# Top-10 indices of 8192 rows: smaller chunks, keys in planes, merged gathers and an order by hand

## The chip, the cores and the metric

One core of a Trainium2 chip. The metric is the device time of one execution in microseconds (us), the median of the runs that a comparison made; the granted clock was 1.00. "Before" and "after" are the two kernels of the change. In the profile, SPq is the queue of SyncE, which issues the DMAs; DVE is VectorE, ACT is ScalarE, POOL is GpSimd.

## The reference

```python
x = np.random.randn(8192, 8192).astype(np.float32)      # k = 10
indices = np.argpartition(x, -k, axis=1)[:, -k:]
values = np.take_along_axis(x, indices, axis=1)
sorted_idx = np.argsort(-values, axis=1)
return np.take_along_axis(indices, sorted_idx, axis=1)  # 8192 x 10 indices, largest first
```

The input is 268 MB, read once; 64 tiles of 128 rows.

## The kernel before

Per tile: load 4 MB (two halves), convert to fp16 keys on ScalarE, fold each chunk of 16 keys to its maximum on VectorE, choose the 12 best chunks of 512, gather those chunks in fp32 on GpSimd, separate them, rank the 192 candidates. Each of the four gathers writes 768 values a row (the page's line L134): 16 sets of 3 chunks of 16, one set for each row of its group of 16, so each row needs only its own; sixteen small DMAs per tile pick it out.

```python
C = 16; G = 12; LAG = 2                                 # NCHUNK = 8192 // C
def load(t):                                            # cut: tile 0 in eight parts
    for h in range(2):
        nc.sync.dma_start(out=xt[:, h*w:(h+1)*w], in_=x[r0:r0+P, h*w:(h+1)*w])

def front(t):
    for h in range(2):
        kh = kpool.tile([P, H], fp16, tag="kh")
        nc.scalar.activation(out=kh, in_=xt[:, h*H:(h+1)*H], func=ACTF.Copy, bias=-CENTER)   # dense
        v = kh.rearrange("p (c w) -> p c w", w=C)
        n = C // 2
        while n > 1:                                    # folds in place, short runs
            nc.vector.tensor_tensor(out=v[:, :, 0:n], in0=v[:, :, 0:n], in1=v[:, :, n:2*n], op=ALU.max)
            n //= 2
        nc.vector.tensor_tensor(out=m[:, h*HC:(h+1)*HC], in0=v[:, :, 0], in1=v[:, :, 1], op=ALU.max)
    # choice: max, max_index, match_replace, max, max_index on m [128, 512]
    nc.scalar.activation(out=idx[:, :, 0:3], in_=cid[:, 0:G]..., func=ACTF.Copy, scale=float(C))
    gw = gwpool.tile([P, G, 16, C], fp32, tag="gw")
    for s in range(0, G, 3):                            # four gathers of 48 indices
        nc.gpsimd.indirect_copy(out=gw[:, s:s+3]..., data=xt..., idxs=idx[:, s//3, 0:3])
    for r in range(16):                                 # each row's own set, 8 partitions a copy
        nc.sync.dma_start(out=g[r::16, :, :], in_=gw[r::16, :, r, :])
# back(t): five VectorE instructions on g; every 8th tile decode() and one output DMA, on SyncE
for t in range(ntiles):                                 # the scheduler orders the rest
    load(t); front(t)
    if t >= LAG: back(t - LAG)
```

## Time and profile before

| | before |
|---|---|
| median (lowest to highest) | 1241.06 us (1240.95 to 1242.26, 3 runs) |
| busy share VectorE / ScalarE / GpSimd | 65% / 39% / 27% |
| mean load rate | 217 GB/s; 359 GB/s while a load runs |
| mean time from load to load, SyncE's timeline, 54.27 to 1169.18 us | 18.9 us |

The busy shares alone say nothing here: no engine is full. In a wait line the three numbers are the total us, the number of times and the longest.

### The profile page before, as it was taken

How to read it: one execution, taken by the hardware profiler on the slowest of the kernel's cores; microseconds unless marked ns; L12 is line 12 of the kernel's file. 1: busy time of each engine (PE TensorE's matmuls, PEld its weight loads, DVE VectorE, ACT ScalarE, POOL GpSimd, SP SyncE). 2: the span in 40 equal slices, each digit the busy share in tenths (PEclk: the TensorE clock that was granted, in tenths of full speed). 3: DMA queues.
4: the chain of work that ended last, by engine and by line, in shares of the span. 5: the costliest groups of instructions: out<-in, count | busy, mean ns of one | idle time of the engine just before them, and what ended most of it. 6: DMA issues, size and time to landing. Idle time of an engine off the chain costs nothing.

```text
span 1241.8 us, 4178 instructions
## 1 busy us (share of the span) xinstructions
PE 0.2 (0%) x2; PEld 0.1 (0%) x2; DVE 804.0 (65%) x1589; ACT 478.9 (39%) x199; POOL 339.0 (27%) x263
## 2 busy tenths in 40 slices
PE   0000000000000000000000000000000000000000
PEld 0000000000000000000000000000000000000000
DVE  5866666766766657666676567756667576685642
ACT  6344343343343443333443433424433334334310
POOL 0222223222222222222232222222222223223221
DMA  9656656557556566465575575565664765656610
GB/s 393 236 204 263 235 199 259 201 217 275 215 203 258 192 242 257 167 270 217 208 269 200 218 274 207 212 234 201 258 255 164 276 222 202 267 180 239 265 17 8
DMA packets 134146, 275.70 MB, mean 222 GB/s; under 512 B 116960, under 2 KB 116960, under 8 KB 117984
## 3 DMA queue, kind: packets, MB, share of 16 engines
q1 hardware_dynamic: 134112, 275.42, 59.8%
q14 instruction: 34, 0.28, 0.1%
HBM read 268.44 MB, written 0.66 MB: 217 GB/s over the span
## 4 chain that ended last, share of the span: by engine, by line
DMA 54%; SPq 29%; DVE 8%; issue 5%; ACT 2%; POOL 1%; POOLq 0%; DVEq 0%; PE 0%; ACTq 0%
DMA xt<-in_x_dram 54%; SPq L142 27%; ACT kh L95 2%; SPq L80 2%; DVE kh L103 2%; DVE pick L178 1%; DVE hot L170 1%; POOL gw L134 1%; DVE cidb L119 0%; DVE hot L174 0%; DVE wall L122 0%; DVE wall L118 0%; DVE m L120 0%; DVE m L107 0%; DVE posb L155 0%
## 5 line engine op out<-in xcount | busy, mean ns | idle before, releaser
L103 DVE TENSOR_TENSOR kh<-kh 128x2048 f16<-128x2048 f16 (+2 forms) x384 | 342.2, 891 | 377.4 <-ACT kh L95 368.7
L134 POOL INDIRECT_COPY gw<-xt,idx 128x768 f32 x256 | 338.3, 1322 | 880.5 <-issue 630.0
L95 ACT ACTIVATE kh<-xt 128x4096 f16<-128x4096 f32 (+1 forms) x134 | 464.2, 3464 | 267.8 <-DMA xt<-in_x_dram 267.7
L127 ACT ACTIVATE idx<-cidb 128x12 uint16<-128x12 uint16 x64 | 13.7, 214 | 445.2 <-DVE cidb L123 445.2
L107 DVE TENSOR_TENSOR m<-kh 128x256 f16<-128x256 f16 x128 | 85.8, 671 | 4.4
L122 DVE MAX8 wall<-m 128x8 f16<-128x512 f16 x64 | 44.5, 695 | 2.2
L118 DVE MAX8 wall<-m 128x8 f16<-128x512 f16 x64 | 44.5, 695 | 2.2
L151 DVE MAX8 t8a<-g 128x8 f32<-128x192 f32 x64 | 22.0, 344 | 33.8 <-DMA g<-gw 33.5
L119 DVE FIND_INDEX8 cidb<-wall,m 128x8 uint16<-128x512 f16 x64 | 43.8, 685 | 0.0
L123 DVE FIND_INDEX8 cidb<-wall,m 128x8 uint16<-128x512 f16 x64 | 43.8, 685 | 0.0
L120 DVE MATCH_REPLACE8 m<-wall,m 128x512 f16<-128x512 f16 x64 | 43.2, 676 | 0.0
L154 DVE MAX8 t8b<-g 128x8 f32<-128x192 f32 x64 | 23.1, 361 | 2.2
L155 DVE FIND_INDEX8 posb<-t8b,g 128x8 uint16<-128x192 f32 x64 | 22.5, 352 | 0.0
L152 DVE FIND_INDEX8 posb<-t8a,g 128x8 uint16<-128x192 f32 x64 | 22.5, 352 | 0.0
L153 DVE MATCH_REPLACE8 g<-t8a,g 128x192 f32<-128x192 f32 x64 | 21.9, 343 | 0.0
L170 DVE TENSOR_TENSOR hot<-slot,slots 128x960 f16<-128x960 uint16 x8 | 9.5, 1190 | 0.0
L178 DVE TENSOR_REDUCE pick<-hot 128x80 f32<-128x960 f16 x8 | 9.2, 1153 | 0.3
L155 DVE MATCH_VALUE_LOAD posb<-t8b,g 128x8 f32 x64 | 5.9, 92 | 2.2
L123 DVE MATCH_VALUE_LOAD cidb<-wall,m 128x8 f16 x64 | 5.9, 92 | 2.2
L152 DVE MATCH_VALUE_LOAD posb<-t8a,g 128x8 f32 x64 | 5.9, 92 | 2.2
L119 DVE MATCH_VALUE_LOAD cidb<-wall,m 128x8 f16 x64 | 5.9, 92 | 2.2
L174 DVE TENSOR_TENSOR hot<-hot,cidb 128x960 f16<-128x960 f16 x8 | 5.8, 722 | 0.3
(19 smaller groups left out, 21.7 us busy)
## 6 DMA issues: line engine op xcount, KB each, us to landing
xt<-in_x_dram SPq DMA_DIRECT2D x126, 2048.0 KB
g<-gw SPq DMA_DIRECT2D x1024, 6.0 KB
xt<-in_x_dram SPq DMA_DIRECT2D x8, 512.0 KB
out_dram<-opack SPq DMA_DIRECT2D x8, 80.0 KB
```

What stands on the lines that cost most here:

```text
L95: nc.scalar.activation(out=kh[:, q * w:(q + 1) * w], in_=xt[:, h * H + q * w:h * H + (q + 1) * w], func=ACTF.Copy, bias=-CENTER, scale=1.0,)
L103: nc.vector.tensor_tensor(out=v[:, :, 0:n], in0=v[:, :, 0:n], in1=v[:, :, n:2 * n], op=ALU.max)
L107: nc.vector.tensor_tensor(out=m[:, h * HC:(h + 1) * HC], in0=v[:, :, 0], in1=v[:, :, 1], op=ALU.max)
L118: nc.vector.max(out=w16[:, 0:8], in_=m)
L119: nc.vector.max_index(out=cid[:, 0:8], in_max=w16[:, 0:8], in_values=m)
L120: nc.vector.match_replace(out=m2, in_to_replace=w16[:, 0:8], in_values=m, imm_value=KEY_MIN)
L122: nc.vector.max(out=w16[:, 8:16], in_=m2)
L123: nc.vector.max_index(out=cid[:, 8:16], in_max=w16[:, 8:16], in_values=m2)
L134: nc.gpsimd.indirect_copy(out=gw[:, s:s + per, :, :].rearrange("p s r w -> p (s r) w"), data=xt.rearrange("p (c w) -> p c w", w=C), idxs=i ...
L142: nc.sync.dma_start(out=g[r::16, :, :], in_=gw[r::16, :, r, :])
L152: nc.vector.max_index(out=pos[:, 0:8], in_max=t8a, in_values=g)
L155: nc.vector.max_index(out=pos[:, 8:16], in_max=t8b, in_values=g2)
```

## The change

Its intent: chunks of 8 halve the candidates to rank and the words that a gather reads; keys stored plane by plane (all first elements, then all second ones) make every fold one contiguous run; two gathers replace four; the gather buffer is laid out so that each row's set is one run; the output DMA leaves SyncE's queue; and the order is set by hand, with the next tile's conversion ahead of this tile's index. The cut leaves out the numbers of buffers: the key buffers go from three half tiles to two whole ones, and the small tiles from three buffers to two.

```diff
-C = 16
+C = 8
+PER = 6
-            ... kh = kpool.tile([P, H], fp16), converted dense, in two halves, folded in place
+        khs[t] = kpool.tile([P, C, NCHUNK], fp16, tag="kh", name="kh")
+            nc.scalar.activation(
+                out=khs[t][:, :, h * w // C:(h + 1) * w // C],
+                in_=xt[:, h * w:(h + 1) * w].rearrange("p (c w) -> p w c", w=C),
+                func=ACTF.Copy, bias=-CENTER, scale=1.0)
+        n = N // 2                                     # fold(t)
+        while n >= NCHUNK:
+            nc.vector.tensor_tensor(out=kh[:, 0:n], in0=kh[:, 0:n], in1=kh[:, n:2 * n], op=ALU.max)
+            n //= 2
-        gw = gwpool.tile([P, G, 16, C], fp32, tag="gw")           # four gathers
+        gw = gwpool.tile([P, 16, G, C], fp32, tag="gw")
+        for a in range(G // PER):                                 # two gathers of 96 indices
+            ... mybir.InstIndirectCopy(..., num_valid_indices=16 * PER)
-            nc.sync.dma_start(out=g[r::16, :, :], in_=gw[r::16, :, r, :])
+            nc.sync.dma_start(out=gs[t][r::16, :], in_=gw[r::16, r, :, :]...)
-        nc.sync.dma_start(out=out_tpn...)
+        nc.scalar.dma_start(out=out_tpn...)
+    with tc.manual_schedule():
+        for t in range(3): load(t)
+        convert(0)
+        for t in range(ntiles + LAG):
+            if t < ntiles:
+                fold(t); choose(t)
+                if t + 1 < ntiles: convert(t + 1)
+                index(t)                               # ScalarE, behind convert(t + 1)
+                gather(t)                              # two gathers, then 16 copies on SyncE
+                if t + 3 < ntiles: load(t + 3)         # SyncE, behind the copies of t
+            if t >= LAG: rank(t - LAG)
```

More of the change, by code (lines that the diff above doesn't have):

```diff
@@ L50 @@
     consts = ctx.enter_context(tc.tile_pool(name="consts", bufs=1))
-    kpool = ctx.enter_context(tc.tile_pool(name="keys", bufs=3))
+    kpool = ctx.enter_context(tc.tile_pool(name="keys", bufs=2))
     gwpool = ctx.enter_context(tc.tile_pool(name="gw", bufs=2))
-    small = ctx.enter_context(tc.tile_pool(name="small", bufs=3))
+    small = ctx.enter_context(tc.tile_pool(name="small", bufs=2))
     bpool = ctx.enter_context(tc.tile_pool(name="batch", bufs=2))
@@ L69 @@
         nc.gpsimd.memset(o, 0)
-    st = {}
-    batch = {}
+    xts, khs, gs, idxs, batch = {}, {}, {}, {}, {}
+    H = N // 2
     def load(t):
-        xt = xpool.tile([P, N], fp32, tag="xt")
+        xts[t] = xpool.tile([P, N], fp32, tag="xt", name="xt")
         r0 = t * P
@@ L80, in load, with convert, fold, choose @@
             nc.sync.dma_start(
-                out=xt[:, h * w:(h + 1) * w], in_=x[r0:r0 + P, h * w:(h + 1) * w]
+                out=xts[t][:, h * w:(h + 1) * w], in_=x[r0:r0 + P, h * w:(h + 1) * w]
             )
-        st[t] = {"xt": xt}
-    def front(t):
-        xt = st[t]["xt"]
-        m = small.tile([P, NCHUNK], fp16, tag="m")
-        H = N // 2
-        HC = NCHUNK // 2
-        for h in range(2):
-            kh = kpool.tile([P, H], fp16, tag="kh")
-            nparts = 4 if t == 0 else 1
-            w = H // nparts
-            for q in range(nparts):
-                nc.scalar.activation(
-                    out=kh[:, q * w:(q + 1) * w],
-                    in_=xt[:, h * H + q * w:h * H + (q + 1) * w],
-                    func=ACTF.Copy, bias=-CENTER, scale=1.0,
-                )
-            v = kh.rearrange("p (c w) -> p c w", w=C)
-            n = C // 2
-            while n > 1:
-                nc.vector.tensor_tensor(
-                    out=v[:, :, 0:n], in0=v[:, :, 0:n], in1=v[:, :, n:2 * n], op=ALU.max
-                )
-                n //= 2
+    def convert(t):
+        xt = xts[t]
+        khs[t] = kpool.tile([P, C, NCHUNK], fp16, tag="kh", name="kh")
+        nparts = 8 if t == 0 else 2
+        w = N // nparts
+        for h in range(nparts):
+            nc.scalar.activation(
+                out=khs[t][:, :, h * w // C:(h + 1) * w // C],
+                in_=xt[:, h * w:(h + 1) * w].rearrange("p (c w) -> p w c", w=C),
+                func=ACTF.Copy, bias=-CENTER, scale=1.0,
+            )
+    def fold(t):
+        kh = khs[t].rearrange("p w c -> p (w c)")
+        n = N // 2
+        while n >= NCHUNK:
             nc.vector.tensor_tensor(
-                out=m[:, h * HC:(h + 1) * HC], in0=v[:, :, 0], in1=v[:, :, 1], op=ALU.max
+                out=kh[:, 0:n], in0=kh[:, 0:n], in1=kh[:, n:2 * n], op=ALU.max
             )
+            n //= 2
+    def choose(t):
+        m = khs.pop(t)[:, 0, :]
         if t % TB == 0:
@@ L116, in front @@
         w16 = wall[:, t, :]
-        m2 = small.tile([P, NCHUNK], fp16, tag="m2")
         nc.vector.max(out=w16[:, 0:8], in_=m)
         nc.vector.max_index(out=cid[:, 0:8], in_max=w16[:, 0:8], in_values=m)
+        m2 = small.tile([P, NCHUNK], fp16, tag="m2")
         nc.vector.match_replace(out=m2, in_to_replace=w16[:, 0:8], in_values=m,
@@ L123, in front, with index, gather, rank @@
         nc.vector.max_index(out=cid[:, 8:16], in_max=w16[:, 8:16], in_values=m2)
-        per = 3
-        idx = small.tile([P, G // per, 4], u16, tag="idx")
+    def index(t):
+        cid = batch[t // TB][0][:, t % TB, :]
+        idxs[t] = small.tile([P, G // PER, 8], u16, tag="idx", name="idx")
         nc.scalar.activation(
-            out=idx[:, :, 0:per],
-            in_=cid[:, 0:G].rearrange("p (a b) -> p a b", b=per),
+            out=idxs[t][:, :, 0:PER],
+            in_=cid[:, 0:G].rearrange("p (a b) -> p a b", b=PER),
             func=ACTF.Copy, scale=float(C),
         )
-        gw = gwpool.tile([P, G, 16, C], fp32, tag="gw")
-        for s in range(0, G, per):
-            nc.gpsimd.indirect_copy(
-                out=gw[:, s:s + per, :, :].rearrange("p s r w -> p (s r) w"),
-                data=xt.rearrange("p (c w) -> p c w", w=C),
-                idxs=idx[:, s // per, 0:per],
-                i_know_this_is_slow=True,
+    def gather(t):
+        gw = gwpool.tile([P, 16, G, C], fp32, tag="gw")
+        for a in range(G // PER):
+            runs = gw[:, :, a * PER:(a + 1) * PER, :].rearrange("p r s w -> p s r w")
+            nc.gpsimd.add_instruction(
+                mybir.InstIndirectCopy(
+                    name=nc.get_next_instruction_name(),
+                    ins=[nc.gpsimd.lower_ap(xts[t]), nc.gpsimd.lower_ap(idxs[t][:, a, 0:PER])],
+                    outs=[nc.gpsimd.lower_ap(runs)],
+                    num_valid_indices=16 * PER,
+                )
             )
-        g = small.tile([P, G, C], fp32, tag="g")
+        gs[t] = small.tile([P, G * C], fp32, tag="g", name="g")
         for r in range(16):
-            nc.sync.dma_start(out=g[r::16, :, :], in_=gw[r::16, :, r, :])
-        st[t]["g"] = g
-    def back(t):
-        g = st.pop(t)["g"].rearrange("p s w -> p (s w)")
+            nc.sync.dma_start(
+                out=gs[t][r::16, :], in_=gw[r::16, r, :, :].rearrange("p s w -> p (s w)")
+            )
+        del xts[t], idxs[t]
+    def rank(t):
+        g = gs.pop(t)
         pos = batch[t // TB][1][:, t % TB, :]
@@ L182, in decode @@
         )
-        nc.sync.dma_start(
+        nc.scalar.dma_start(
             out=out_tpn[:, b * TB:(b + 1) * TB, :],
@@ L186, in decode @@
         )
-    for t in range(ntiles):
-        load(t)
-        front(t)
-        if t >= LAG:
-            back(t - LAG)
-    for t in range(ntiles - LAG, ntiles):
-        back(t)
+    with tc.manual_schedule():
+        for t in range(3):
+            load(t)
+        convert(0)
+        for t in range(ntiles + LAG):
+            if t < ntiles:
+                fold(t)
+                choose(t)
+                if t + 1 < ntiles:
+                    convert(t + 1)
+                index(t)
+                gather(t)
+                if t + 3 < ntiles:
+                    load(t + 3)
+            if t >= LAG:
+                rank(t - LAG)
     tie = small.tile([P, ntiles], fp32, tag="tie")
```

## The prediction

> **What bounds the kernel now.** I read the page first: the busy shares, then the chain that ended last, because no engine is near full.
>
> ```profile
> PE 0.2 (0%) x2; PEld 0.1 (0%) x2; DVE 804.0 (65%) x1589; ACT 478.9 (39%) x199; POOL 339.0 (27%) x263
> ...
> DMA 54%; SPq 29%; DVE 8%; issue 5%; ACT 2%; POOL 1%; POOLq 0%; DVEq 0%; PE 0%; ACTq 0%
> ```
>
> VectorE is idle a third of the time and the chain is made of input loads (54%) and of SyncE's own queue (29%), so this is a loop between the loads and the queue that issues them. Next, the timeline of SyncE over one of the 64 tiles:
>
> ```profile
> 601.03 0.86 SPq L80 DMA_DIRECT2D xt<-in_x_dram  x2
> 602.00 17.05 SPq L142 DMA_DIRECT2D g<-gw  x16
> 619.16 0.86 SPq L80 DMA_DIRECT2D xt<-in_x_dram  x2
> ```
>
> From one pair of loads to the next is 18.1 us. The chain of waits over the same stretch says why 16 small copies take 17 us:
>
> ```profile
> 601.46 11.83 DMA xt<-in_x_dram
> 613.29 0.02 issue
> 613.30 0.60 SPq L142
> 613.90 0.04 issue
> ...
> 618.45 0.60 SPq L142
> 619.05 0.06 issue
> ```
>
> [...]copies 7 and 8 after a load pair wait for the two halves of that load. SyncE issues seven copies in the load's shadow, waits until it lands (613.29), then issues nine more at 0.643 us, and only then the next load. The period is 12.3 (load issue to landing) + 9 x 0.643 + about 0.1 = 18.2. The same two stretches, by windows (us, then busy time of each engine, clock, DMA share, GB/s):
>
> ```profile
> 601.50:613.30 11.80, 0.00 (x0) 0.00 (x0) 7.35 (x19) 3.83 (x2) 3.80 (x3) 1.00 0.93 359
> 613.30:619.60 6.30, 0.00 (x0) 0.00 (x0) 4.69 (x6) 3.62 (x1) 1.25 (x1) 1.00 0.09 8
> ```
>
> Full rate while the load runs, 8 GB/s while nine copies are issued: bandwidth is not the limit. Finally the instructions that the change touches, from the groups with shapes kept apart:
>
> ```profile
> L95 ACT ACTIVATE kh<-xt 128x4096 f16<-128x4096 f32 x126 | 455.7, 3617 | 263.8 <-DMA xt<-in_x_dram 263.7
> L134 POOL INDIRECT_COPY gw<-xt,idx 128x768 f32 x256 | 338.3, 1322 | 880.5 <-issue 630.0 <-DMA g<-gw 248.3 <-ACT idx L127 2.2
> L103 DVE TENSOR_TENSOR kh<-kh 128x2048 f16<-128x2048 f16 x128 | 161.3, 1260 | 368.7 <-ACT kh L95 368.7
> ...
> L107 DVE TENSOR_TENSOR m<-kh 128x256 f16<-128x256 f16 x128 | 85.8, 671 | 4.4
> L122 DVE MAX8 wall<-m 128x8 f16<-128x512 f16 x64 | 44.5, 695 | 2.2
> ...
> L154 DVE MAX8 t8b<-g 128x8 f32<-128x192 f32 x64 | 23.1, 361 | 2.2
> ```
>
> An indirect_copy shows 1.3 us busy but 2.2 us of "issue" before it. In the timeline of the tail, where nothing else runs, four of them start at 1208.43, 1211.89, 1215.35 and 1218.81: one costs 3.46 us, so a tile's four 13.8 us.
>
> [...] The trace agrees that 8-partition copies are the dear ones:
>
> ```profile
> L142 SPq DMA_DIRECT2D g<-gw x1024: 589/599/5939, 43.9 to 1229.8; - x171
> L183 SPq DMA_DIRECT2D out_dram<-opack x8: 394/394/411, 194.7 to 1237.5; - x8
> ```
>
> The output copy has 1,024 runs of 80 bytes and costs 0.394 us of issue; the separating copy has 96 runs and costs 0.599. Runs do not set the issue cost. [...]L107 reads one fp16 per 32 bytes and takes 671 ns for 256 elements, where the dense rate seen in MAX8 ((695-361)/(512-192), about 1.04 ns an element) would add only 267 ns to an overhead of some 150 ns[...]. [...]the gap before an indirect_copy grows from 2.2 to 3.8 us where folds run. [...]
>
> **The change part by part.**
> (1) Folds. [...]2048 outputs take 1.26 us now, so 4096 take 1.26+1.07 = 2.33, 1024 take 0.73; sum 4.3 us a tile, against 2 x (1.260+0.742+0.671+0.671) = 6.7. Saves 2.4.
> (2) Chunk choice. 1024 maxima instead of 512: five instructions, each 512 x 1.04 = 0.53 us longer: +2.7. Ranking has 96 elements instead of 192: 5 x -0.1 = -0.5. VectorE's work a tile stays near 12.6 us (804/64) and it is not the bound.
> (3) Conversion. ScalarE now reads fp32 with a step of 32 bytes[...]. Dense: 3.617 = 0.20 + 4096 x 0.833 ns. [...]0.20 + 4096 x 1.667 = 7.0 us a half. I give this three chances in four.
> (4) Gathers. Two instructions with 96 indices of 8 elements: the written 768 elements stay, 1.26 us each. The 2.2 us gap stays if it is a cost per instruction and becomes 4.4 if per index; I choose the middle, 3.3. Two cost 2 x (3.3+1.26) = 9.1 us instead of 13.8.
> (5) Separation. Still 16 copies over 8 partitions: I keep 0.643 us each. 96 runs become 8, which only lightens DMA work that the 359 GB/s shows to be harmless.
> (6) Output copy on ScalarE's queue. SyncE's waits list 76.9 us for VectorE's decode. Counting load pairs, 54.3 to 1169.2 us holds 59 periods, mean 18.9; the plain ones are 18.1 to 18.8, so some 4 us for each of seven batches, about 30 us, is really saved.
> (7) Order. This is the part I fear. The manual order puts the index instruction of tile t behind the conversion of t+1 on ScalarE, and the load of t+3 behind the copies of t on SyncE. So load(t+1), conversion(t+1), index(t), gathers(t), copies(t), load(t+3) is one chain over two periods. Before, the index came straight after the choice, the gathers ran beside a whole load, and four tiles were prefetched, not three. Moreover fold(t+1) starts at the same moment as gathers(t) and holds them off: 4.3 us, less about 1.1 us which the gather seems to get done first (at 22.02 the index is there, the folds end at 25.45, writing starts at 26.58, only 1.1 later), so about 3.0.
>
> Two periods are: the first half's conversion starts 7.4 us after the load's issue (608.39-601.03), two conversions 14.1, index 0.3, gathers 3.0+9.1, 16 copies 10.3, waits 0.2: 44.4 us, so 22.2 us a tile. Head: conversion of tile 0 in eight pieces of 1.9 ends at 20, of tile 1 at 34, gathers 46, copies and load(3) at 56.5. Then 60 periods, 1332. Tail from the last load: conversion 21.5, index 21.8, gathers of the last two tiles 33.9 and 43.0, copies to 54.5, landing 1.8, ranking to end 10.1 as now: 66. Sum 56.5+1332+66 = 1455.
>
> **Rivals.** (a) ScalarE reads at full rate. Then conversion ends 12.3+3.7 after the load's issue, and two periods are 16.0+0.4+12.1+10.5 = 39.0, 19.5 a tile; head 49, tail 61: 1280. For it: the conversion writes densely and reads one stream. Against: L107.
> (b) The gather gap is a cost per instruction (2.2). That takes 2 x 1.1 us off two periods: 21.1 a tile and about 1385; with (a) 18.4, close to the queue bound, about 1210.
> (c) The queue bound of 12.3 + 9 copies stays the only limit and the batches' stalls go: 18.2 x 60 + head 49 + tail 61 = 1202. It needs both (a) and (b).
> (d) Longer runs cut the issue of a copy to 0.39 us. Sixteen save 3.3 us in two periods: 1455 becomes 1355, and (c) would fall to some 16.3 a tile, near 1090. Against: the output copy above.
> (e) The gap is fully per index (4.4): 23.3 a tile, about 1525.
>
> **Range and chances.** Strided ScalarE at 3 in 4 spans 1385 to 1525; dense ScalarE mostly 1210 to 1310. I put the time a little under the main sum, 1430, because several small rivals pull down and one up; 1250 to 1510 should hold it 8 times in 10. Faster needs two or three rivals at once: 0.10. Within 2%: 0.13. Slower: 0.77.
>
> **What would show it.** The conversion's mean for 4096 elements (7.0 or 3.6 us); the start-to-start time of the two indirect_copies without folds (4.6, or 3.5, or 5.7); the issue of a separating copy (0.60 or 0.39); SyncE waiting mainly for GpSimd and no longer for loads; load pairs alternating short and long with a mean near 22 us; the index waiting on ScalarE's own order. A dense conversion makes the number wrong; SyncE still waiting for the loads makes the mechanism wrong.

The marked cuts here and in the expectations are what no trace or run of this case shows. No term of the sum goes with them: two periods still come to 44.4 us and the whole to 1455. What is left rests on the traces as follows.

- That copies 7 and 8 wait for the two halves of a load is in SyncE's timeline: after the load pair of 601.03, copy 6 starts at 605.24, copy 7 at 608.33 and copy 8 at 613.30, with two waits for the load in between, 4.0 us in all. What in the queue makes them wait is not shown.
- The folds' 1.07 us for 2048 more outputs is an estimate: about twice the step from 1024 to 2048 outputs, 742 to 1260 ns.
- The 7.0 us is an estimate too, under an "if": that ScalarE pays twice its dense 0.833 ns for each element, as L107 on VectorE takes (671 - 150)/256 = 2.03 ns an element against MAX8's 1.04. The 150 ns are rounded from 695 - 512 x 1.04 = 162.

## The result, and the profile after

| | before | after |
|---|---|---|
| median | 1241.66 us (4 runs) | 1491.24 us (4 runs, 1490.61 to 1491.63) |
| ratio, 95% interval | | 1.2003 (1.1978 to 1.2027) |
| VectorE / ScalarE / GpSimd busy | 65% / 39% / 27% | 53% / 65% / 10% |
| mean time from load to load | 18.9 us | 22.8 us |

A ratio here is the mean time of one kernel's runs over that of the other's of the same rounds, so not quite the ratio of the medians. The mean time from load to load is the last issue of a load pair less an early one in SyncE's timeline, over the pairs between (after: 1423.37 - 75.97 us over 59).

From the page of the changed kernel, the busy line and the chain that ended last:

```profile
PE 0.2 (0%) x2; PEld 0.1 (0%) x2; DVE 787.5 (53%) x1269; ACT 968.3 (65%) x199; POOL 147.0 (10%) x135
...
SPq 37%; issue 31%; DMA 20%; POOL 9%; DVE 1%; ACT 1%; POOLq 0%; DVEq 0%; PE 0%; ACTq 0%
```

The loads' own share of the chain fell from 54% to 17% (the page's line list; the other 3% of DMA are copies landing): what now fills it is the copies' issue (SPq) and the gathers with the unshown part in front of them (issue and POOL). ScalarE has 1% of this chain, so the profile does not put the conversion on it; that the conversion is on the path is read from the times below and shown by experiment 1. What SyncE waits for says the same, from its queue's waits:

```profile
SPq L146 <- POOL gw L136: 766.7, 63, 38.6
...
SPq L146 <- DMA xt<-in_x_dram: 3.7, 2, 2.8
```

Before, it waited 181 us for loads and 101 us for GpSimd; now 4 and 767. The queue's old bound, copies 7 and 8 waiting for a load to land, hardly binds any more. Two periods of the timeline of the changed kernel, from one load pair to the second one after it (start, duration, engine, line, operation):

```profile
603.92 0.85 SPq L81 DMA_DIRECT2D xt<-in_x_dram  x2
...
611.34 14.96 ACT L91 ACTIVATE kh<-xt 128x4096 f16<-128x4096 f32 x2 [10.56 <-DMA xt<-in_x_dram]
...
626.21 0.20 ACT L126 ACTIVATE idx<-cidb 128x12 uint16<-128x12 uint16 x1
626.34 4.28 DVE L101 TENSOR_TENSOR kh<-kh 128x4096 f16<-128x4096 f16 x3 [13.57 <-ACT kh L91]
...
633.71 1.14 POOL L136 INDIRECT_COPY gw<-xt,idx 128x768 f32 x1 [19.70 <-issue]
...
638.49 1.15 POOL L136 INDIRECT_COPY gw<-xt,idx 128x768 f32 x1 [3.64 <-issue]
639.66 9.63 SPq L146 DMA_DIRECT2D g<-gw  x16
...
649.40 0.85 SPq L81 DMA_DIRECT2D xt<-in_x_dram  x2
```

Read it downwards: each step begins where the one above ends (the L101 line is no step of the chain: it is the fold that starts with the index). The load leads to the conversion of tile t+1, that to the index of tile t (whose choice had been ready since 611), that to the gathers, those to the copies, those to the next load but one: 649.40 - 603.92 = 45.5 us for two tiles. The shown part of the first gather, which I take to be its writing, starts 7.3 us after the index ends (626.41), that of the second only 3.64 after the first: the fold that starts with the index held the first back. Experiment 2 has the control: no fold runs there between the index and the next gather, and the wait is 3.8 us. Note that the profile calls the 19.70 us "issue": it shows no wait, though the index had come only 7.3 us before. As the prediction said they would, the load pairs alternate short and long: 18 to 21 us and 25 to 28.

The groups with shapes kept apart, after:

```profile
L91 ACT ACTIVATE kh<-xt 128x4096 f16<-128x4096 f32 x126 | 945.2, 7552 | 475.2 <-DMA xt<-in_x_dram 475.2
L101 DVE TENSOR_TENSOR kh<-kh 128x4096 f16<-128x4096 f16 x64 | 146.7, 2293 | 655.7 <-ACT kh L91 655.7
L136 POOL INDIRECT_COPY gw<-xt,idx 128x768 f32 x128 | 146.3, 1143 | 1321.8 <-issue 1293.5 <-DMA xt<-in_x_dram 24.5 <-DVE posb L161 3.8
```

The strided conversion takes 7.55 us a half against 3.62; the largest fold and the gather's shown part are as cheap as hoped.

### The profile page after: what moved, and what is told of

The parts are those of the page before. It is cut to its first block, busy times and chain, and to the rows that moved or that the text cites. A ratio compares the mean times of both kernels' runs of the same rounds, so it can differ in the third digit from the quotient of the medians.

```text
span 1489.7 us, 3606 instructions
## 1 busy us (share of the span) xinstructions
PE 0.2 (0%) x2; PEld 0.1 (0%) x2; DVE 787.5 (53%) x1269; ACT 968.3 (65%) x199; POOL 147.0 (10%) x135
## 4 chain that ended last, share of the span: by engine, by line
SPq 37%; issue 31%; DMA 20%; POOL 9%; DVE 1%; ACT 1%; POOLq 0%; DVEq 0%; PE 0%; ACTq 0%
SPq L146 37%; DMA xt<-in_x_dram 17%; POOL gw L136 9%; DMA g<-gw 3%; ACT kh L91 1%; SPq L81 0%; DVE kh L101 0%; POOLq L136 0%; DVE cidb L116 0%; DVE wall L120 0%; DVE wall L115 0%; DVE m L118 0%; DVE pick L184 0%; DVE hot L176 0%; DVE hot L180 0%
## 5 line engine op out<-in xcount | busy, mean ns | idle before, releaser
L91 ACT ACTIVATE kh<-xt 128x4096 f16<-128x4096 f32 (+1 forms) x134 | 960.6, 7222 | 477.6 <-DMA xt<-in_x_dram 477.6
L101 DVE TENSOR_TENSOR kh<-kh 128x4096 f16<-128x4096 f16 (+2 forms) x192 | 269.8, 1405 | 660.1 <-ACT kh L91 655.7
L136 POOL INDIRECT_COPY gw<-xt,idx 128x768 f32 x128 | 146.3, 1143 | 1321.8 <-issue 1293.5
L120 DVE MAX8 wall<-m 128x8 f16<-128x1024 f16 x64 | 78.6, 1228 | 2.2
L115 DVE MAX8 wall<-kh 128x8 f16<-128x1024 f16 x64 | 78.6, 1228 | 2.2
L116 DVE FIND_INDEX8 cidb<-wall,kh 128x8 uint16<-128x1024 f16 x64 | 78.0, 1219 | 0.0
L121 DVE FIND_INDEX8 cidb<-wall,m 128x8 uint16<-128x1024 f16 x64 | 78.0, 1219 | 0.0
L118 DVE MATCH_REPLACE8 m<-wall,kh 128x1024 f16<-128x1024 f16 x64 | 77.4, 1209 | 0.0
L160 DVE MAX8 t8b<-g 128x8 f32<-128x96 f32 x64 | 16.7, 261 | 2.1
L158 DVE FIND_INDEX8 posb<-t8a,g 128x8 uint16<-128x96 f32 x64 | 16.1, 252 | 0.0
```

The lines of the kernel that those rows point to most:

```text
L91: nc.scalar.activation(out=khs[t][:, :, h * w // C:(h + 1) * w // C], in_=xt[:, h * w:(h + 1) * w].rearrange("p (c w) -> p w c", w=C), fun ...
L101: nc.vector.tensor_tensor(out=kh[:, 0:n], in0=kh[:, 0:n], in1=kh[:, n:2 * n], op=ALU.max)
L115: nc.vector.max(out=w16[:, 0:8], in_=m)
L116: nc.vector.max_index(out=cid[:, 0:8], in_max=w16[:, 0:8], in_values=m)
L118: nc.vector.match_replace(out=m2, in_to_replace=w16[:, 0:8], in_values=m, imm_value=KEY_MIN)
L120: nc.vector.max(out=w16[:, 8:16], in_=m2)
```

## The experiments

My theory: in the order by hand, load(t+1), conversion(t+1), index(t), gathers(t), copies(t) and load(t+3) form one chain over two tiles, so half of every step in it is paid per tile, the slow conversion included. The rivals: the slow conversion alone did it; the order alone did it; the gathers' instructions are the bound; the copies' runs set their cost. All runs were timed in three rounds against the kernel before on the same chip; all gave correct results except the first. Each ratio stands with its 95% interval.

**1. Dense conversion, wrong result.** Edit on the changed kernel (the folds then compare the wrong elements; their time is the same):

```diff
-                out=khs[t][:, :, h * w // C:(h + 1) * w // C],
-                in_=xt[:, h * w:(h + 1) * w].rearrange("p (c w) -> p w c", w=C),
+                out=khs[t].rearrange("p w c -> p (w c)")[:, h * w:(h + 1) * w],
+                in_=xt[:, h * w:(h + 1) * w],
```

> Wrong result on purpose: the conversion of the changed kernel reads and writes densely, so the folds compare the wrong elements; everything else, the order included, stays. My theory (the two-period chain load, conversion, index, gathers, copies, load, with a strided conversion in it): a half conversion falls from 7.55 to 3.62 us, two periods from 45.5 to 16.0 + 0.3 + 13.2 + 9.8 + 0.1 = 39.4 us, and the time to about 1290 us, still slower than before. Rival 'the order alone does it and the conversion is hidden': stays near 1490. Rival 'the stride is all of it': 1240 or less.

Measured: 1291.43 us, ratio 1.0409 (1.0392 to 1.0426); the conversion took 3.616 us a half; mean period 19.6 us (expected 19.7). The slow conversion is worth 200 us in this order, and without it the changed kernel is still slower than before. So the conversion alone did not do it, and in the changed kernel the order alone did not either.

**2. The index on VectorE.** It is 12 values a row; done on VectorE behind the choice, it no longer queues behind the next conversion:

```diff
-        nc.scalar.activation(out=idxs[t][:, :, 0:PER], in_=cid[:, 0:G]..., func=ACTF.Copy, scale=float(C))
+        nc.vector.tensor_scalar(out=idxs[t][:, :, 0:PER], in0=cid[:, 0:G]...,
+            scalar1=C.bit_length() - 1, scalar2=None, op0=ALU.logical_shift_left)
...
-                if t + 1 < ntiles: convert(t + 1)
-                index(t)
+                index(t)
+                if t + 1 < ntiles: convert(t + 1)
```

> The changed kernel with the index multiplication moved from ScalarE to VectorE, straight behind the choice; the strided conversion stays at 7.55 us a half. My theory: the chain now spans three periods, 22.6 (load and conversion) + 4.3 + 6.4 + 0.4 + 11.6 + 9.8 = 55 us, 18.3 us a tile, near the queue bound of 12.3 + 9 x 0.602 = 17.9, so about 1220 us. Rival 'the slow conversion costs the time wherever it stands': 1400 to 1490. Rival 'the gathers are the bound': unchanged.

Measured: 1275.22 us, ratio 1.0278 (1.0261 to 1.0295), with the conversion as slow as ever (7.574 us). One 0.2 us instruction in another queue gives back 216 of the 250 us, which also ends the rival that the gathers are the bound: it would have left the time unchanged. My number was 55 us too low, and the queue's waits show a term that I had not counted:

```profile
SPq L146 <- POOL gw L136: 376.9, 56, 33.9
SPq L146 <- DMA xt<-in_x_dram: 101.1, 37, 4.9
SPq L146 <- DMA out_dram<-opack: 87.9, 7, 13.0
```

Behind the output DMA of a batch a copy waits until that DMA has landed, which it cannot before VectorE has decoded the batch: seven stalls, 88 us in all, not all of it on the path. Why a copy waits for it is not shown.

The same run has the control for the fold that holds a gather back. From its timeline, an index, the first gather after it, and the next fold:

```profile
604.46 0.17 DVE L126 TENSOR_SCALAR idx<-cidb 128x12 uint16<-128x12 uint16 x1
...
608.40 1.14 POOL L136 INDIRECT_COPY gw<-xt,idx 128x768 f32 x1 [8.10 <-issue]
...
615.18 4.28 DVE L101 TENSOR_TENSOR kh<-kh 128x4096 f16<-128x4096 f16 x3 [8.82 <-ACT kh L91]
```

With no fold in the way the gather shows 608.40 - 604.63 = 3.77 us after the index, against 7.30 in the changed kernel.

**3. The order alone.** The changed kernel's order with all the parts of the kernel before: chunks of 16, dense conversion, in-place folds, four gathers, 96 runs a copy (a rewrite of those functions; the loop is the changed kernel's own). Three things stay as in the changed kernel: its numbers of buffers, the conversion of a whole tile ahead of its folds, and the output DMA on ScalarE's queue. No wait in this trace, or in the changed kernel's, is for a free key or small buffer, so the buffers are not the cause.

> The kernel before (chunks of 16, dense conversion, four gathers, 96 runs a copy) in the changed kernel's manual order: index of t behind the conversion of t+1, load of t+3 behind the copies of t. My theory: two periods 16.0 + 0.3 + 13.8 + 2 (folds in the way) + 10.3 + 0.2 = 42.6, 21.3 us a tile, about 1400 us. Rival 'the order is harmless, the strided conversion did it': about 1210 to 1240.

Measured: 1503.30 us, ratio 1.2117 (1.2097 to 1.2137): the order costs the kernel before 262 us with no slow conversion in it, 100 more than I expected. In its queue's timeline a load pair and the second one after it are 45.3 us apart (610.73 to 656.01), not 42.6. An index ends at 626.95; the gathers that follow it, from the timeline of GpSimd:

```profile
631.50 1.25 POOL L144 INDIRECT_COPY gw<-xt,idx 128x768 f32 x1 [16.92 <-issue]
634.98 1.25 POOL L144 INDIRECT_COPY gw<-xt,idx 128x768 f32 x1 [2.23 <-issue]
638.46 1.25 POOL L144 INDIRECT_COPY gw<-xt,idx 128x768 f32 x1 [2.23 <-issue]
644.35 1.25 POOL L144 INDIRECT_COPY gw<-xt,idx 128x768 f32 x1 [4.65 <-issue]
```

From the index's end to the last gather's end is 18.65 us: the work is 4 x 3.46 = 13.8, and 2.3 and 2.4 us are lost, at the first gather to one fold (2.76 us from 626.87) and at the fourth to the fold of a later half tile (2.76 us from 640.19). I had counted one such collision. That is 2.8 us in two periods, most of the miss.

**4. Scatter the writes in place of the reads.** The same planes, with the conversion reading densely and writing with a step of 2 KB:

```diff
+                out=khs[t][:, :, ...].rearrange("p w c -> p c w"),
+                in_=xt[:, h * w:(h + 1) * w].rearrange("p (c w) -> p c w", w=C),
```

> Correct result: the changed kernel with the conversion's loops swapped, so that it reads densely and scatters its fp16 writes over the eight planes. If only the strided read costs[...]: 3.6 us a half and about 1290 us, as e1. If a strided write costs as much: 7 us or more and about 1490 us or more.

Measured: 2377.84 us, ratio 1.9163 (1.9131 to 1.9195).

```profile
L91 ACT ACTIVATE kh<-xt 128x4096 f16<-128x4096 f32 x126 | 2292.2, 19516 | 0.0
```

A half takes 19.5 us from start to end and ScalarE never waits: it is the bound. The next half starts before the last has ended (busy 2292.2 us for 126), so one half costs 18.2 us and an element 18.2/4096 = 4.4 ns, against 1.8 ns with the strided read and 0.83 dense. My expectation for the costly case (7 us or more, 1490 us or more) was far too mild.

**5. The order taken away.** `with tc.manual_schedule():` becomes `if True:`.

> The changed kernel with the manual order taken away, so that the scheduler orders it; no other edit. The built order puts the index of a tile behind that tile's own conversion and ahead of the next one, as in the kernel before. My theory: with a strided conversion this is a serial chain on ScalarE, 15.1 (conversion) + 4.3 + 6.3 (folds, choice) + 0.5 = 26.2 us a tile, about 1700 us: the order by hand was needed because of the slow conversion. Rival 'the order by hand is the fault in itself': 1250 or less.

Measured: 1682.60 us, ratio 1.3572 (1.3549 to 1.3594). The waits of ScalarE show the serial chain:

```profile
ACT idx L126 <- DVE cidb L121: 667.3, 62, 11.4
```

The scheduler put the index of a tile ahead of the next conversion, and ScalarE stands for 11 us a tile until the choice is made. With a conversion of 15 us a tile that is ScalarE's whole time (its timeline repeats every 26.1 us: indices at 606.05 and 632.13). So the order by hand was not simply bad: it beats the scheduler's by 191 us on this conversion. Either place on ScalarE's queue is wrong; experiment 2 took the index off it.

**6. Four gathers at chunks of 8.** `PER = 3` in place of 6.

> The changed kernel with four gathers of 48 indices in place of two of 96, chunks still of 8. If a gather costs by indices and elements (what I now think, as the gap went from 2.20 to 3.63 us with twice the indices of half the size): about 1.8 + 0.57 = 2.4 us each, 9.5 us a tile as with two, and the time stays within 1% of 1491. If each instruction has a fixed cost that the change halved: a gap of 2.2 us or more, 11.1 us or more a tile, and 1535 us or more.

Measured: 1518.98 us, ratio 1.2255 (1.2235 to 1.2276), between the two forecasts. From the end of its GpSimd timeline, where little else runs:

```profile
1487.93 0.82 POOL L136 INDIRECT_COPY gw<-xt,idx 128x384 f32 x1 [1.73 <-issue]
1490.48 0.82 POOL L136 INDIRECT_COPY gw<-xt,idx 128x384 f32 x1 [1.73 <-issue]
```

One gather of 48 indices of 8 elements costs 2.55 us, four 10.2; two of 96 cost 2 x 4.78 = 9.6; four of 48 indices of 16 cost 13.8. So halving the chunk saved 3.6 us a tile and merging the instructions 0.6. The gap before the writing doubles with the indices (1.73 to 3.63): it is work per index, not a fee per instruction. The 28 us by which this kernel is slower than the changed one are 0.43 us a tile (in the chain half of 0.6 is 0.3; the rest I have not traced).

**7. One run per row alone.** The kernel before with its gather buffer laid out `[P, 16, G, C]` and nothing else changed.

> The kernel before with only its gather buffer relaid, so that a separating copy moves one run of 768 bytes per partition in place of twelve of 64. My theory (the issue is set by the 8 partitions, little by the runs): nine copies behind each load at 0.602 in place of 0.643 us, 0.4 us a tile, about 1217 us. Rival 'the small runs are what makes a copy dear': 0.43 us a copy, nearly 2 us a tile, about 1120 us.

Measured: 1216.56 us, ratio 0.9813 (0.9797 to 0.9830). From the tile's view:

```profile
L145 SPq DMA_DIRECT2D g<-gw x1024: 557/558/789, 44.0 to 1201.5; - x171
```

A copy's issue falls from 0.599 to 0.558 us though its runs fall from 96 to 8; nine copies behind each load, 64 tiles: 9 x 0.041 x 64 = 24 us, as measured. By the rule of 2% the verdict is "unclear", but the interval is clear of 1. The part of the change that is about runs works and is small. Rival (d) of the prediction falls.

**8. A version built on the theory.** From the changed kernel: dense conversion; folds that pack their results; the index on VectorE; load(t+3) ahead of the copies; the copies of two tiles in one set of 16; the output DMA issued one tile later; and ranking three tiles behind in place of two (`LAG = 3`).

```diff
+    def fold(t):                       # kh dense [P, 8192]; results packed at its front
+        n = C
+        while n > 1:
+            v = kh[:, 0:NCHUNK * n].rearrange("p (c w) -> p c w", w=n)
+            n //= 2
+            nc.vector.tensor_tensor(out=kh[:, 0:NCHUNK * n].rearrange("p (c w) -> p c w", w=n),
+                in0=v[:, :, 0:n], in1=v[:, :, n:2 * n], op=ALU.max)
...
-        gw = gwpool.tile([P, 16, G, C], fp32, tag="gw")
+        if t % 2 == 0: pair[t // 2] = gwpool.tile([P, 16, 2, G, C], fp32, tag="gw", name="gw")
...
-                gather(t)              # with its 16 copies
-                if t + 3 < ntiles: load(t + 3)
+                gather(t)
+                if t + 3 < ntiles: load(t + 3)
+                if t + 1 < ntiles: convert(t + 1)
+                if t % 2 == 1: separate(t // 2)        # 16 copies for two tiles
```

> A version built on the theory: chunks of 8 and two gathers as in the change, but a dense conversion, folds that pack their result, the index on VectorE, loads issued ahead of the copies, and the copies of two tiles in one set of 16. If the coupling of loads and copies through SyncE is what bounds both kernels, VectorE becomes the bound with about 5.5 + 6.2 + 0.2 + 1.6 + 0.6 = 14 us a tile and the time is about 980 us (940 to 1050). If something else bounds (the gathers, the load rate), it stays above 1150.

Measured: 956.88 us, ratio 0.7715 (0.7702 to 0.7728): 23% less time than before and 36% less than the changed kernel. From its page:

```profile
PE 0.2 (0%) x2; PEld 0.1 (0%) x2; DVE 840.4 (88%) x1333; ACT 464.9 (49%) x135; POOL 159.9 (17%) x135
```

VectorE is now near its bound, as intended: 840 us of work in 956, and 92% of the stretch from 100 to 850 us. The page's chain still runs mostly through loads (DMA 55%, SPq 19%, DVE 19%), so VectorE is not shown to be the only bound. Of the parts, only the pairs and the early load are taken back one by one below. The packed folds take 2.304, 1.232 and 1.232 us, 0.55 us a tile more than the planes' 2.293, 1.225 and 0.699, and cost ScalarE nothing.

**9. The same without pairs.** One set of 16 copies per tile.

> The best version so far (957 us) with one set of 16 copies per tile again in place of one per two tiles; everything else as in it. My theory: [...]copies 7 and 8 behind a load wait for its landing, so the period is again 12.3 + 9 x 0.602 + 0.1 = 17.8 us and the time about 1190 us, although no engine needs more than 14 us a tile. Rival 'the packed dense folds, the index on VectorE and the early loads made the gain': within 5% of 957.

Measured: 1174.54 us, ratio 0.9472 (0.9456 to 0.9488), as expected.

```profile
SPq L154 <- DMA xt<-in_x_dram: 429.2, 120, 4.9
```

Every load stops the copies twice, as in the kernel before, and its VectorE work is that of experiment 8, no longer the bound. The run doubles the copies of a tile as well as the waits, and the 218 us are for both. But 16 copies at 0.60 us and two loads at 0.43 are 10.5 us a tile, less than VectorE's 13.1, so their number alone does not make the period of 17.9 us: the wait for the load does. In the kernel before it was copies 7 and 8, eight places behind the two halves of a load, that waited (they start at 608.33 and 613.30, the conversions of those halves at 608.39 and 613.37); what makes a copy wait there is not shown, and no run varies it alone.

**10. The early load undone, pairs kept.** load(t+3) behind the copies again.

> The best version with the load of t+3 put behind the copies again, pairs of tiles kept. My theory: the chain now spans four tiles, 22.6 (two loads) + 3.7 + 4.8 + 6.6 + 13.2 + 9.6 = 60.5 us, 15.1 us a tile, about 1010 us. If the place of the load does not matter: 957 as before.

Measured: 1083.16 us, ratio 0.8733 (0.8719 to 0.8748). The place of the load matters (126 us), but my period of 15.1 us was too short by over 1 us a tile; I did not trace what fills it.

The copies in pairs on the kernel before alone stay untested. With chunks of 8 the doubled buffer is as large as the old single one.

## Why the prediction was right

The time, 1491, lies in the range of 1250 to 1510, near its upper end, and slower had 0.77. The mechanism, part (7), holds: the chain over two periods is there link by link in the timeline, and experiments 1, 2 and 3 move it in the direction that it says, 1 to within 2 us, 2 and 3 with misses of 55 and 100 us. Term by term, for two periods:

| term | predicted us | measured us (603.92 to 649.40) |
|---|---|---|
| load issue to the start of conversion | 7.4 | 7.4 |
| two conversions | 14.1 | 15.0 |
| index | 0.3 | 0.1 |
| gathers, with the wait for the fold | 12.1 | 13.2 |
| 16 copies | 10.3 | 9.6 |
| the rest | 0.2 | 0.1 |
| sum | 44.4 | 45.5 |

Head and tail: 56.5 and 66 predicted; 58.1 (the first load behind copies) and 66.3 (1489.7 - 1423.4) measured. The main sum, 1455, was closer than the 1430: shading it down for "several small rivals" was the poorest step, since (a), (b) and (d) all failed, and (c) with (a) and (b).

- Part (1), right: folds 4.22 us a tile (2.293 + 1.225 + 0.699; predicted 4.3). Part (2), right: the five choice instructions grew from about 0.69 to 1.22 us each, 2.7 in all.
- Part (3), right in kind, a little small: 7.55 instead of 7.0 us a half; (7.55 - 0.20)/4096 is 1.79 ns an element, 2.15 dense elements' time. Rival (a) falls; experiment 4 adds that writing with a step of 2 KB is worse, and does not tell whether the writing or the larger step makes it so. There was some luck in the factor of two: the prediction held L107's 2.03 ns an element against MAX8's 1.04. Dense folds of the same kind take (1260 - 742)/1024 = 0.51 ns, so on VectorE the strided form costs four times the dense one, not twice.
- Part (4), a middle chosen without knowledge: the gap is 3.63 us (predicted 3.3) and the writing 1.14 (predicted 1.26), 4.78 together instead of 4.56. Rival (b) falls. Rival (e) had the kind right and the size wrong: with chunks of 8 the gap doubles with the indices (1.73 to 3.63, experiment 6), but halved chunks make each index cheaper (2.20 to 1.73), which no one had counted. That the middle came so close is luck.
- The fold in the way: 7.30 - 3.77 = 3.5 us instead of 3.0 (3.77 from experiment 2), the other part of the gathers' miss.
- Part (5), right that runs hardly matter, with 0.04 us a copy that I had put at nothing. It is why the copies' term was too large.
- Part (6): after the change SyncE's waits no longer list the decode. The 30 us were not isolated, and the estimate was high: of the 59 periods the 52 plain ones are 18.1 to 19.2 us, mean 18.5, and the seven with a batch average 21.9, so 24 us in all. Experiment 2 shows that the output DMA can stall SyncE's queue all the same (seven waits, 87.9 us).
- What the prediction did not say: how the causes weigh. The order alone is enough to make the kernel before slower, by 262 us (3); with the other parts but a dense conversion it is 1291 (1), so smaller gathers, cheaper copies and the rest give back 212; the slow conversion takes 200. These add up along this path only: on the automatic order the same conversion makes 1683 (5), with the index elsewhere 1275 (2).

## What to carry to other kernels

Before moving an instruction within an engine's queue, write down the ring it closes: here a tiny index behind the next tile's conversion (its choice ready at 611, the index run at 626.21) tied two tiles into one chain, and every slow part was then paid through it. Look in the queue's waits for small copies that wait for a large load: here for one issued eight DMAs earlier (181 us in the kernel before, 429 in experiment 9), and issuing fewer small DMAs (one set for two tiles) cut that to 93 us and the time from 1175 to 957 us, where cheaper ones barely moved the time (ratio 0.981). The layout that made VectorE's folds contiguous moved the stride to ScalarE's conversion (7.55 us a half against 3.62); packing the result of each fold left that pass dense (3.62) and cost VectorE 0.55 us a tile.
